# A decoder layer with sparse attention: the sample cache's compression written into the attention loop, one batch per pair, with the key and value ring over its memory

## The chip, the cores and the metric

The kernel runs on one core of one Trainium2 chip. The metric is device microseconds of one execution, as the median of several runs. Lower is better.

## What is computed

One layer of a hybrid decoder for 1024 prompt tokens and 8 sample sequences of 4 new tokens, with 2048 tokens of paged cache behind each sequence. The model width is 1024; there are 8 query heads and 2 key/value heads of 64. Everything is float32; the large products are made as three products of a high and a low part each.

```python
# both token sets (prompt, sample)
u, v_n, q_n, q_r, kcr, vcr, ks, vs, kw, vw, gate, mg = in_projection(rms_norm(x))
o_a = gmlp_mix(u, v_n, w_s, b_s)              # mixer A, chunks of 128 tokens
kc = rms_norm(compress(kc_rows, w_ck1, w_ck2, pe_k))   # 32 rows -> 1, stride 16
vc = compress(vc_rows, w_cv1, w_cv2, pe_v)
# mixer B: three softmaxes per query: compressed blocks, selected blocks, window of 512
o_b = g0 * att(q_n, kc, vc) + g1 * att(q_r, top 16 blocks) + g2 * att(q_r, window)
x = x + (sigmoid(g_a) * (o_a @ w_a) + sigmoid(g_b) * (o_b @ w_b)) @ w_out
x = x + square(relu(rms_norm(x) @ w_up)) @ w_down
...
def compress(rows, w1, w2, pe):               # rows in chunks of 16 tokens
    first, second = ch @ w1[:half], ch @ w1[half:]
    return gelu(first[:, :-1] + second[:, 1:] + pe @ w1) @ w2
```

For the prompt the rows of `compress` are made in the kernel. For the samples they are the pages of two caches, 16 pages of 128 tokens for each of 8 sequences, found through a page table. The selected and window branches of the samples read further caches in the same way.

## The kernel before

The program is one straight list of tiles and operations. A scheduler orders the instructions of each engine from it: what stands earlier in the program has the higher priority, `tc.high_priority()` lifts what it encloses, and later work is placed where an engine would otherwise be idle. On the chip each engine then runs its own list in order, so an instruction that waits holds all that stand behind it. `tc.manual_schedule(engines={SP})` fixes, for SyncE (SP), the order in which the enclosed instructions are written; other SP instructions may be placed between them. Pools of on-chip memory are a stack: a pool opened after another was released lies over its bytes, and each new tile waits for the tiles that it covers.

The stages are these. First come the projections of keys, values, gates, mixer A and the queries, until about 233 us.

Then comes the prompt attention, in 32 steps that the code calls `pairs`: 8 blocks of 128 queries times 4 pairs of heads (loop over `u`, from line 889). Pair `u` of query block qb works on 2*(qb+1) + 2*min(qb+1, 5) + 1 blocks of 128 keys, in chunks of four, 560 blocks in all; pairs 20 to 31 hold 300 of them. One step of the loop does the logits and softmax of pair `u` (`a_steps`: TensorE to bank S, VectorE maxima, ScalarE exponentials, GpSimd scaling) and, between those, the transposes and value products of pair `u-1` (`c_steps`: `T` to bank PT, `PV` to bank O, `E` at its end). `E` stores the result to `o_d` with an SP DMA (line 873). `q_trans(u + 1)` transposes the next pair's queries and at its end issues the load of the pair two further on (`q_load`, two SP DMAs).

The compression of the sample caches follows in the program (from line 958): 16 items, 8 sequences for the keys and then 8 for the values. An item loads 16 pages of 64 KB (`c_load`; SP loads 16 page numbers into registers in two `TENSOR_LOAD`s, line 923, then issues 16 DMAs, line 931) into `raw`, of which there are two. In four quarters it splits `raw` into `hl` (one ScalarE copy, one subtraction on GpSimd, or on VectorE for the first quarter) and makes six products with `w1s` into bank F, of which there is one. A chain of small operations (`comp_hidden`, `comp_out`, for keys also `comp_knorm`) ends in the copy `co`, which GpSimd stores to `c_d`. The page loads stand in a manual order of their own; the scheduler places query loads and `o_d` stores between them.

After that stand 12 blocks of a projection that depend on nothing in the attention (`fillers(W0, ...)`, 36 chunks of 24 matmuls of 352 columns into the one bank G, weights `whl` split by ScalarE and GpSimd). They serve as filling: lowest in priority, they take what TensorE has free.

The sample attention is next. The top-k part ranks the compressed blocks (`kct` is read back from `c_d`, `q_pad` spreads the sample queries, the result is `smask`). Then ten steps of `kv_load` bring 2 MB each into `ring` (two buffers, lines 1105 to 1111), with logits, softmax and values for each; another 24 chunks of filling (`fill(W1, ...)`) stand between them. The weights of W1 lie over the prompt's keys and values (pool `kvp`, released after the attention). In memory, the pools `pa` (compression) and `p2` (attention) are released together, and `fp` (filling), `ps3` (top-k) and `p3` (ring and sample softmax) lie over them, in that order.

Branch products, output projection and the MLP follow, from about 880 us to the end.

Of the kernel before, what the change touches and what calls it, by code (L numbers as in the profile page):

```python
# [26 lines left out]
NRB = 2  # L27
# [8 lines left out]
N3 = 0  # L36
# [9 lines left out]
def build(tc, a):  # L46
# [783 lines left out]
    def c_steps(u, chunks, Ps):  # L830
# [32 lines left out]
        def E():  # L863
# [9 lines left out]
            SP.dma_start(o_d[4 + pr, :, qb * 128:(qb + 1) * 128], o)  # L873

        return T, PV, E

    hp = tc.high_priority()
    hp.__enter__()
    q_load(0)
    q_load(1)  # L880
    q_trans(0)
    prev = None
    for u in range(len(pairs) + 1):
        if u == HPU:
            hp.__exit__(None, None, None)
        A, C = [], 0
        if prev:
            pu, pch, pPs = prev
            T, PV, E = c_steps(pu, pch, pPs)
            C = len(pch)  # L890
            T(0)
            T(1)
        if u < len(pairs):
            chunks, Ps, A = a_steps(u)
            prev = (u, chunks, Ps)
            A.pop(0)()
            q_trans(u + 1)
        n_a = len(A)
        for c in range(C):
            PV(c)  # L900
            T(c + 2)
            k = min(n_a, -(-n_a * (c + LEAD) // C))
            while A and n_a - len(A) < k:
                A.pop(0)()
        while A:
            A.pop(0)()
        if C:
            E()

# [48 lines left out]
    cl = Ahead([lambda w=w, b=b: c_load(w, b) for w in range(2) for b in range(8)], RAWA)  # L958
    ctxm = tc.manual_schedule(engines={mybir.EngineType.SP})
    ctxm.__enter__()  # L960
    for which in range(2):
        w1, bias, w2 = c_weights(which)
        for b in range(8):
            raw = cl()
            tg = "FG"[b % 2] if which * 8 + b < N3 else "F"
            pb = bank(tg, 1, psS)
            out = pb[:, 0:256].rearrange("p (k g r) -> p k g r", k=2, r=8)
            for qt in range(4):
                hl = pa.tile([128, 2, 16, 32], F32R, name="hl", bufs=HIB)
                cols = slice(qt * 32, (qt + 1) * 32)  # L970
                with tc.high_priority():
                    cp(hl[:, 0], raw[:, :, cols])
                    (POOL if qt else DVE).tensor_tensor(hl[:, 1], raw[:, :, cols], f(hl[:, 0]), op=OP.subtract)
                hv, lv = (hl[:, i].rearrange("p g (o k r) -> p o k g r", k=2, r=8) for i in range(2))
                for o in range(2):
                    mm(out, w1[:, 0, qt * 2 + o], hv[:, o], qt + o == 0, False)
                    mm(out, w1[:, 1, qt * 2 + o], hv[:, o], False, False)
                    mm(out, w1[:, 0, qt * 2 + o], lv[:, o], False, qt == 3 and o == 1)
            with tc.high_priority():
                g = comp_hidden(pb[:, 0:256].rearrange("p (k c) -> p k c", k=2), 128, bias, pa)  # L980
                pb2 = bank(tg, 1, psS)
                comp_out(pb2[:, 0:128], g, w2)
                if which == 0:
                    z = comp_knorm(pb2[:, 0:128], pa, gkc, 1)
                    pt = bank(tg, 1, psS)
                    PE.transpose(pt[:, 0:128], z, ident)
                    pb2 = pt
                co = small([128, 128], "co", 1, p=pa)
                cp(co, pb2[:, 0:128])
                POOL.dma_start(c_d[which, b], co)  # L990
# [563 lines left out]
```

## Time and profile before

| | us |
|---|---|
| median of 3 runs | 1826.92 |
| lowest, highest | 1823.32, 1830.13 |
| the profiled execution's own time | 1824.63 |
| its span, first to last instruction | 1822.9 |

| stretch of the profiled execution (us) | what runs |
|---|---|
| 0 to 233 | projections |
| 233 to 704 | prompt attention, compression, filling W0, top-k of the samples at its end |
| 704 to 880 | sample attention with filling W1 |
| 880 to 1823 | branch products, output projection, MLP |

The profile's page gives the busy time of each engine over the span; the windows view gives it for each stretch, with the clock that TensorE was granted (1.00 is 2.4 GHz, a mean between 0.50 and 1.00 is a mix of that and 1.2 GHz). The timeline lists an engine's instructions in order, and in brackets the idle time before one and what ended it. Matmul durations overlap, so the cost of one in a row of many is the stretch divided by the count.

### The profile page before, as it was taken

Reading aid. Unit: us, or ns where it says so; the run is one execution under the profiler, and the core shown is the slowest. Engines: PE = TensorE matmul, PEld = TensorE weight load, DVE = VectorE, ACT = ScalarE, POOL = GpSimd, SP = SyncE. Lnnn points to the kernel's source line nnn. Section 1 sums busy time; section 2 is a strip of 40 time slices with the busy share of each in tenths; the row PEclk is TensorE's granted clock in tenths of the full one; section 3 lists DMA queues with packets and bytes.
Section 4 is the critical chain, followed back from the end, with each engine's and each line's share of the span. In section 5 each row is a group of like instructions: output and inputs, shape, how many; then the busy total and the mean of one; then the engine's idle time right before and its main releaser. Section 6 shows DMA issues by size and latency. Waiting matters only on the chain.

```text
span 1822.9 us, 30327 instructions
## 1 busy us (share of the span) xinstructions
PE 1754.0 (96%) x11095; PEld 1655.3 (91%) x11095; DVE 939.5 (52%) x2371; ACT 701.7 (38%) x1681; POOL 411.3 (23%) x603
## 2 busy tenths in 40 slices
PE   8999989999999987999899999999999999999999
PEld 6877879999999965667899999999999999999998
DVE  7637867867777884124664454333333333333333
ACT  5534567777677772222422333201320122003300
POOL 3103456665566543222000220000000000000000
PEclk9999999999999997999999999999999999999999
DMA  6232453333333224665543221111111111111121
GB/s 200 94 98 64 132 161 107 112 104 96 117 89 87 70 62 143 198 188 192 176 152 108 91 70 47 47 47 47 45 38 46 47 47 47 47 47 47 47 84 59
DMA packets 157703, 168.71 MB, mean 93 GB/s; under 512 B 51825, under 2 KB 132338, under 8 KB 157554
## 3 DMA queue, kind: packets, MB, share of 16 engines
q1 hardware_dynamic: 140194, 135.77, 24.0%
q0 software_dynamic: 6464, 20.19, 3.3%
q10 hardware_dynamic: 10896, 10.82, 1.9%
q8 instruction: 87, 1.43, 0.3%
q14 instruction: 62, 0.51, 0.1%
HBM read 136.54 MB, written 29.13 MB: 91 GB/s over the span
## 4 chain that ended last, share of the span: by engine, by line
PE 83%; DVE 7%; SPq 3%; DMA 2%; ACT 2%; issue 2%; POOL 1%; ACTq 0%; DVEq 0%; POOLq 0%
PE S L73 27%; PE G L73 18%; PE PT L73 14%; PE F L73 10%; PE O L73 10%; PE PT L843 2%; SPq L931 2%; DVE PH L57 1%; SPq L923 1%; DMA ol<-o_d 1%; DMA ring<-cs 1%; DVE S L773 1%; PE PT L698 1%; ACT P L782 0%; DMA xr<-xT 0%
## 5 line engine op out<-in xcount | busy, mean ns | idle before, releaser
L73 PE MATMUL G<-big,whl 128*128 128x352 f32 x1440 | 271.1, 333 | 14.6 <-ACT whl L54 7.0
L73 PEld LDWEIGHTS G<-big,whl 128*128 128x128 f32 x1440 | 235.5, 191 | 43.4 <-issue 16.5
L54 ACT ACTIVATE whl<-wraw 128x1024 fp32r<-128x1024 f32 x100 | 106.1, 1061 | 429.7 <-PE S L73 145.8
L73 PE MATMUL S<-U,whl 128*128 128x352 f32 x864 | 201.6, 324 | 0.0
L73 PE MATMUL S<-H,whl 128*128 128x352 f32 x840 | 190.5, 324 | 0.0
L73 PE MATMUL PT<-U,whl 128*128 128x352 f32 x576 | 154.9, 324 | 0.0
L73 PEld LDWEIGHTS S<-U,whl 128*128 128x128 f32 x864 | 150.1, 188 | 0.0
L797 POOL TENSOR_SCALAR P<-P,rs 128x128 f32<-128x128 f32 (+4 forms) x272 | 132.1, 501 | 77.6 <-DVE rs L57 51.0
L73 PEld LDWEIGHTS S<-H,whl 128*128 128x128 f32 x840 | 145.0, 188 | 0.0
L73 PE MATMUL PT<-H,whl 128*128 128x352 f32 x528 | 143.2, 324 | 0.0
L782 ACT ACTIVATE P<-S,nm 128x512 f32<-128x512 f32 (+3 forms) x208 | 108.8, 532 | 24.7 <-DVE nm L57 16.8
L73 PE MATMUL S<-wt,big 128*128 128x512 f32 x408 | 104.0, 402 | 10.5 <-ACT wt L54 7.4
L57 DVE TENSOR_TENSOR PH<-PT,PH 128x512 fp32r<-128x512 f32 (+2 forms) x160 | 98.5, 618 | 28.4 <-ACT PH L54 27.7
L118 DVE TENSOR_TENSOR whl<-wraw,whl 128x1024 fp32r<-128x1024 f32 x80 | 97.8, 1222 | 14.9 <-ACT whl L54 14.9
L73 PEld LDWEIGHTS PT<-U,whl 128*128 128x128 f32 x576 | 103.3, 188 | 0.0
L73 PE MATMUL O<-PH,V 128*128 128x256 f32 x528 | 94.2, 301 | 9.3 <-DVE PH L57 9.1
L73 PE MATMUL S<-KT,QT 128*128 128x128 f32 (+3 forms) x416 | 97.6, 347 | 4.0 <-ACT P L782 3.0
L54 ACT ACTIVATE PH<-PT 128x512 fp32r<-128x512 f32 (+2 forms) x160 | 86.6, 545 | 38.4 <-PE PT L843 37.3
L73 PE MATMUL F<-H,whl 128*128 128x352 f32 x312 | 101.2, 325 | 0.0
L73 PEld LDWEIGHTS S<-wt,big 128*128 128x128 f32 x408 | 76.2, 191 | 27.4 <-ACT wt L54 7.4
L73 PE MATMUL O<-H,whl 128*128 128x352 f32 x312 | 99.1, 324 | 0.0
L73 PE MATMUL G<-H,whl 128*128 128x352 f32 x312 | 97.6, 325 | 0.5 <-DVE r L1389 0.5
(371 smaller groups left out, 3754.8 us busy)
## 6 DMA issues: line engine op xcount, KB each, us to landing
wraw<-wfm SPq DMA_DIRECT2D x80, 512.0 KB, 3.2
ring<-cs SPq DMA_DIRECT2D x128, 128.0 KB, 2.2
wraw<-wfm POOLq DMA_DIRECT2D x20, 512.0 KB, 4.2
tg<-th_d SPq DMA_DIRECT2D x48, 176.0 KB, 2.8
qdl<-qd_d SPq DMA_DIRECT2D x64, 128.0 KB, 2.6
raw<-cck SPq DMA_DIRECT2D x128, 64.0 KB, 1.9
raw<-ccv SPq DMA_DIRECT2D x128, 64.0 KB, 2.0
wtr<-wtok SPq DMA_DIRECT2D x24, 256.0 KB, 2.7
```

Source lines behind the costliest of these rows:

```text
L54: return ACT.activation(out, in_, AF.Copy, scale=scale)
L57: return DVE.tensor_tensor(out, x, y, op=op)
L73: return PE.matmul(out, l, r, start=start, stop=stop, skip_group_check=skip)
L118: (POOL if i < FM_BR else DVE).tensor_tensor(t[:, 1], raw, f(t[:, 0]), op=OP.subtract)
L698: PE.transpose(pt[:, j], src[:, j], ident)
L773: DVE.tensor_tensor_reduce(S, S, m, scale=-1.0, scalar=3e38, op0=OP.add, op1=OP.min, accum_out=dst)
L782: ACT.activation(Ps[c][:, lo:hi], Ss[c][:, lo:hi], AF.Exp, bias=nm[:, 0, k:k + 1], scale=todo[h, br, i], accum_out=sm[:, i, k:k + 1])
L797: POOL.tensor_scalar(P, P, rs[:, 1, k:k + 1], 1.0, op0=OP.mult, op1=OP.mult)
L843: PE.transpose(pt[:, j], Ps[c][:, j * 128:(j + 1) * 128], ident)
L923: _, vals = nc.values_load_multi_w_load_instructions(ptab[0:1, i0:i0 + 16], engines=[mybir.EngineType.SP], min_val=0, max_val=159, skip_ru ...
L931: SP.dma_start(dst, src)
```

## The change

Four things are changed. The compression item becomes a function `c_item(which, b)`, and the attention loop calls it at the end of step `u` for `u` from 2 to 17, so that item `u - 2` stands in the program behind pair `u`'s logits and ahead of pair `u + 1`. The manual order of SP now begins ahead of the attention loop and encloses it, with its query loads and the page loads in the order in which they are written. The `o_d` store of `E` goes from SP to GpSimd (32 DMAs of 64 KB). And `ring` gets a pool of its own, `rg`, opened first after `pa` and `p2` are released and so at the beginning of `pa`'s memory; `fp`, `ps3` and `p3` follow behind it. The second bank for early items, `N3`, was zero before and goes. The code of `page`, `page_load`, `Ahead`, `c_load` and `c_weights` is only moved.

```diff
@@ c_steps, E @@
-            SP.dma_start(o_d[4 + pr, :, qb * 128:(qb + 1) * 128], o)
+            POOL.dma_start(o_d[4 + pr, :, qb * 128:(qb + 1) * 128], o)
@@ ahead of the attention loop @@
+    ptab = consts.tile([1, 128], I32, name="ptab")
+    SP.dma_start(ptab, a["pt"])
...
+    cl = Ahead([lambda w=w, b=b: c_load(w, b) for w in range(2) for b in range(8)], RAWA)
+    cw = {}
+
+    def c_item(which, b):
+
+        if b == 0:
+            cw[which] = c_weights(which)
+        w1, bias, w2 = cw[which]
+        raw = cl()
+        pb = bank("F", 1, psS)
...
+            co = small([128, 128], "co", 1, p=pa)
+            cp(co, pb2[:, 0:128])
+            POOL.dma_start(c_d[which, b], co)
+
+    ctxm = tc.manual_schedule(engines={mybir.EngineType.SP})
+    ctxm.__enter__()
     hp = tc.high_priority()
     hp.__enter__()
     q_load(0)
@@ end of the loop body @@
         if C:
             E()
...
-    ctxm = tc.manual_schedule(engines={mybir.EngineType.SP})
-    ctxm.__enter__()
-    for which in range(2):
-        w1, bias, w2 = c_weights(which)
-        for b in range(8):
-            raw = cl()
-            tg = "FG"[b % 2] if which * 8 + b < N3 else "F"
...
+        if 2 <= u < 18:
+            c_item((u - 2) // 8, (u - 2) % 8)
+
     ctxm.__exit__(None, None, None)
     p2.release()
     pa.release()
@@ memory of the sample stage @@
     olp = pool("olp", side="right")
+    rg = pool("rg")
     fp = pool("fp")
...
-        t = p3.tile([128, 4, 4, 256], F32, name="ring", bufs=NRB)
+        t = rg.tile([128, 4, 4, 256], F32, name="ring", bufs=NRB)
...
     fp.release()
+    rg.release()
     wst0.release()
```

## Rows read from the trace of the kernel before

**Rows 1.** The page's part 1: busy us, share of span, instructions per engine.
```profile
PE 1754.0 (96%) x11095; PEld 1655.3 (91%) x11095; DVE 939.5 (52%) x2371; ACT 701.7 (38%) x1681; POOL 411.3 (23%) x603
```

**Rows 2.** Windows: length, busy us per engine (instructions), granted clock, DMA share, GB/s.
```profile
250.00:470.00 220.00, 212.94 (x1539) 207.87 (x1538) 164.71 (x568) 160.94 (x476) 135.47 (x214) 0.99 0.40 114
470.00:704.00 234.00, 212.91 (x1521) 200.21 (x1519) 182.23 (x572) 164.99 (x480) 135.00 (x226) 0.96 0.28 80
...
656.00:704.00 48.00, 34.23 (x235) 28.99 (x233) 37.43 (x118) 27.20 (x87) 20.00 (x42) 0.86 0.25 69
704.00:716.00 12.00, 7.78 (x47) 6.32 (x46) 1.51 (x6) 3.08 (x5) 7.32 (x7) 0.57 0.80 250
716.00:866.00 150.00, 140.69 (x971) 101.70 (x969) 43.98 (x109) 38.35 (x88) 32.65 (x40) 1.00 0.62 195
```

**Rows 3.** Timeline of TensorE: start, length, operation, count, idle time before it.
```profile
636.79 1.59 PE L73 MATMUL F<-hl,w1s 128*128 128x256 f32 x12
651.55 0.40 PE L73 MATMUL O<-PH,V2C 128*128 128x256 f32 x2
666.10 0.43 PE L73 MATMUL F<-kct,qp 128*32 128x128 f32 x8 [2.26 <-DMA kct<-c_d]
667.49 0.40 PE L73 MATMUL O<-PH,V2C 128*128 128x256 f32 x2
690.61 0.73 PE L73 MATMUL O<-PH,V 128*128 128x256 f32 x4 [2.69 <-DVE PH L57]
703.78 0.40 PE L73 MATMUL O<-PH,V2C 128*128 128x256 f32 x2
707.24 0.95 PE L73 MATMUL G<-big,whl 128*128 128x352 f32 x2 [3.06 <-ACT whl L54]
860.20 4.02 PE L73 MATMUL G<-big,whl 128*128 128x352 f32 x23 [0.18 <-DVE zu L57]
```

**Rows 4.** Tiles G, F's sources and co: median of one, first and last start.
```profile
L57 DVE TENSOR_TENSOR zt<-G,rep x36: 509/518/526, 260.9 to 615.6; 128x352 f32<-128x352 f32 x36
L54 ACT ACTIVATE hl<-raw x64: 614/632/682, 263.5 to 638.8; 128x512 fp32r<-128x512 f32 x64
L973 POOL TENSOR_TENSOR hl<-raw,hl x48: 1266/1284/1306, 264.7 to 642.3; 128x512 fp32r<-128x512 f32 x48
L54 ACT ACTIVATE co<-F x16: 258/277/318, 293.4 to 653.4; 128x128 f32<-128x128 f32 x16
```

**Rows 5.** SP's page loads and query loads: from the line view, then its timeline.
```profile
L923 SPq TENSOR_LOAD <-ptab x48: 967/978/1607, 247.3 to 832.1; - x48
...
248.74 0.88 SPq L931 DMA_DIRECT2D raw<-cck  x2
249.73 0.93 SPq L690 DMA_DIRECT2D qdl<-qd_d  x2
270.56 10.25 SPq L931 DMA_DIRECT2D raw<-cck  x16
452.91 1.08 SPq L690 DMA_DIRECT2D qdl<-qd_d  x2
```

**Rows 6.** Idle time of engines that ended with a raw load: us, times.
```profile
  DMA raw<-cck: 11.0, 3
  DMA raw<-ccv: 6.5, 3
```

**Rows 7.** GpSimd's DMA issues, 232 to 707 us (busy, mean ns) and in the sample stage.
```profile
L990 POOL DMA_DIRECT2D c_d<-co x16 | 9.5, 597 | 8.9 <-ACT co L54 8.7 <-issue 0.2
L1043 POOL DMA_DIRECT2D th_d<-zt x12 | 7.0, 581 | 7.7 <-ACT zt L1042 3.3 <-DMA raw<-ccv 2.7 <-ACT ch_y L448 1.7
L106 POOL DMA_DIRECT2D wraw<-wfm x20: 537/551/769, 247.4 to 801.5; - x20
L1056 POOL DMA_DIRECT2D o_d<-yt x12: 539/544/547, 807.9 to 883.9; - x12
```

**Rows 8.** SP at the end of the attention: timeline, and its longest wait.
```profile
671.34 35.63 SPq L873 DMA_DIRECT2D o_d<-o_o  x3
708.36 1.91 SPq L931 DMA_DIRECT2D ring<-cs  x4
...
SPq L873 <- POOL o_o L872: 72.9, 5, 19.2
```

**Rows 9.** Sample stage: waits for the ring, and the ranking's result with its uses.
```profile
PE S L73 <- DMA ring<-cs: 6.1, 4, 2.5
...
L1224 DVE CUSTOM_DVE_ANT_1 s_P<-S,smask x8: 691/692/693, 723.9 to 841.5; 128x512 f32<-128x512 f32 x8
L1147 DVE TENSOR_SCALAR smask<-cnt x2: 167/172/176, 687.1 to 695.7; 128x30 f32<-128x30 f32 x2
```

More of the change, by code (lines that the diff above doesn't have):

```diff
@@ L35 @@
 FM_LP = FM_BR
-N3 = 0
 LEAD = 1
@@ L872, in E @@
                 POOL.tensor_tensor(o[64 * h:64 * h + 64], t1[0:64, h], t3[:, h], op=OP.add)
-            SP.dma_start(o_d[4 + pr, :, qb * 128:(qb + 1) * 128], o)
+            POOL.dma_start(o_d[4 + pr, :, qb * 128:(qb + 1) * 128], o)
         return T, PV, E
[L877 to L908, printed above, removed]
     ptab = consts.tile([1, 128], I32, name="ptab")
@@ L958, in build @@
     cl = Ahead([lambda w=w, b=b: c_load(w, b) for w in range(2) for b in range(8)], RAWA)
+    cw = {}
[5 more added lines that the diff above has]
+        pb = bank("F", 1, psS)
+        out = pb[:, 0:256].rearrange("p (k g r) -> p k g r", k=2, r=8)
+        for qt in range(4):
+            hl = pa.tile([128, 2, 16, 32], F32R, name="hl", bufs=HIB)
+            cols = slice(qt * 32, (qt + 1) * 32)
+            with tc.high_priority():
+                cp(hl[:, 0], raw[:, :, cols])
+                (POOL if qt else DVE).tensor_tensor(hl[:, 1], raw[:, :, cols], f(hl[:, 0]), op=OP.subtract)
+            hv, lv = (hl[:, i].rearrange("p g (o k r) -> p o k g r", k=2, r=8) for i in range(2))
+            for o in range(2):
+                mm(out, w1[:, 0, qt * 2 + o], hv[:, o], qt + o == 0, False)
+                mm(out, w1[:, 1, qt * 2 + o], hv[:, o], False, False)
+                mm(out, w1[:, 0, qt * 2 + o], lv[:, o], False, qt == 3 and o == 1)
+        with tc.high_priority():
+            g = comp_hidden(pb[:, 0:256].rearrange("p (k c) -> p k c", k=2), 128, bias, pa)
+            pb2 = bank("F", 1, psS)
+            comp_out(pb2[:, 0:128], g, w2)
+            if which == 0:
+                z = comp_knorm(pb2[:, 0:128], pa, gkc, 1)
+                pt = bank("F", 1, psS)
+                PE.transpose(pt[:, 0:128], z, ident)
+                pb2 = pt
+            co = small([128, 128], "co", 1, p=pa)
+            cp(co, pb2[:, 0:128])
+            POOL.dma_start(c_d[which, b], co)
@@ L959, in build @@
     ctxm = tc.manual_schedule(engines={mybir.EngineType.SP})
     ctxm.__enter__()
-    for which in range(2):
-        w1, bias, w2 = c_weights(which)
-        for b in range(8):
-            raw = cl()
-            tg = "FG"[b % 2] if which * 8 + b < N3 else "F"
[L966 to L990, printed above, removed]
@@ new lines, in build @@
+    hp = tc.high_priority()
+    hp.__enter__()
+    q_load(0)
+    q_load(1)
+    q_trans(0)
+    prev = None
+    for u in range(len(pairs) + 1):
+        if u == HPU:
+            hp.__exit__(None, None, None)
+        A, C = [], 0
+        if prev:
+            pu, pch, pPs = prev
+            T, PV, E = c_steps(pu, pch, pPs)
+            C = len(pch)
+            T(0)
+            T(1)
+        if u < len(pairs):
+            chunks, Ps, A = a_steps(u)
+            prev = (u, chunks, Ps)
+            A.pop(0)()
+            q_trans(u + 1)
+        n_a = len(A)
+        for c in range(C):
+            PV(c)
+            T(c + 2)
+            k = min(n_a, -(-n_a * (c + LEAD) // C))
+            while A and n_a - len(A) < k:
+                A.pop(0)()
+        while A:
+            A.pop(0)()
+        if C:
+            E()
+        if 2 <= u < 18:
+            c_item((u - 2) // 8, (u - 2) % 8)
```

## The prediction

> **What bounds the kernel now.** I read the page's engine line first: TensorE is busy 96% of the span, no other engine over 52% [rows 1]. So nothing that only shortens another engine's work can pay; what can is time in which TensorE is idle or runs at its low clock. Behind 880 us the change touches nothing. The windows view therefore comes next, for the stretches that the change touches [rows 2]. From 250 to 470 us TensorE idles 7 us of 220. From 470 to 704 it idles 21 of 234, and 14 of those lie in the last 48 us, where the granted clock is also 0.86. In the 12 us after the attention it idles 4 and the clock is 0.57. In the sample stage, 716 to 866, it idles 9 of 150 at full clock. So the soft place is the end of the attention.
>
> The timeline says why [rows 3]. The last W0 filling chunk is evacuated at 615.6 us and the last compression item at 653.4 [rows 4]; the attention goes on to 703.78 with nothing to put between its steps, and TensorE waits for its own softmax and transposes (2.69 us for a split of VectorE, 2.26 us for the ranking's load). The last chunk of a pair marks the pace without cover: 651.55 to 667.49 us, 15.9 us for 27 blocks, 0.59 us a block.
>
> **Prices.** A filling chunk is 24 matmuls; 23 take 4.02 us with the tail of the last [rows 3], so I take 3.9 us; 36 chunks are 140 us. A compression item has 24 products, 12 in 1.59 us, and with three small ones I take 3.5 us; 16 are 56 us. TensorE's busy time between 250 and 704 us is 425.9 us [rows 2]; without those two and some 5 us for the ranking, 225 us remain for about 545 blocks of attention, 0.41 us a block. The attention's own pace (0.59) is longer than its TensorE work (0.41), so it needs cover to the end, and the order decides whether there is any.
>
> **The items move forward.** Before, they came one in 24.0 us ((653.4 - 293.4) / 15) [rows 4]. Now item u - 2 stands ahead of pair u + 1, so it takes TensorE time that filling had in the first half, and the filling moves to the second. What paces the first half is SP, whose queue is now in written order. An item costs it two register loads of 0.98 us and sixteen page DMAs in 10.25 us, 12.2 us, and a query load 0.95 us [rows 5], so 13.2 us a pair. The first two loads stand in step 2 and start no earlier than now, at 248.74 us, so the query load behind them goes out at 273 us instead of 249.73. From there one in 13.2 us: the load of pair 20 at 273 + 14 * 13.2 = 458, its transposes at 461 us. Now they are at 452.9 us, when SP issues the load that follows them [rows 5]. Up to 461 TensorE has 211 us: 245 blocks of attention are 100 us, the items 56, start-up idle some 10; 45 us are left, 11 chunks. From 461 us there remain 25 chunks (98 us) and 300 blocks (123 us), 221 us, against 300 * 0.59 = 177 us of the attention's own pace. So TensorE binds to the end. 461 + 221 is 682 us; with 4% idle it is 691. I take 688 us instead of 704, **-16 us**. This agrees with the loss that can be refilled: 13.8 us idle and at most 0.14 * 48 = 6.7 us of clock. Bounds: -22 and 0.
>
> **Loads just in time.** Where an engine reached a split before its pages had landed, the engines together idled 11.0 and 6.5 us, three times each [rows 6]. Now SP has hardly any slack against the items, and a ScalarE copy that waits holds the attention's exponentials behind it, then GpSimd, then TensorE. Not shown before in this density; bounds 0 and 14 items at 2 us, 28 us. I take **+6 us**, nearer to zero, since a late item only delays pages by one item and there are two buffers.
>
> **The o_d stores on GpSimd.** 32 issues at 0.58 to 0.60 us [rows 7] are 19 us of GpSimd, which is busy 58 to 62% there [rows 2]. They wait for GpSimd's own additions, so nothing new is waited for; behind each stands the scaling of the next chunk, which the transposes need. I take 0, with filling as cover; if each came onto the path, 28 stores at 0.6 us, 17 us. Below zero it can give nothing by itself. On SP the stores waited up to 19.2 us for their data [rows 8]; in the written order that would hold page and query loads, and this is what the move avoids. The Trainium skill (page "SBUF — State Buffer", section "SBUF: two separate sides") speaks against it: descriptors of a GpSimd DMA are written through a port that VectorE can hold, and its example takes about 3100 ns instead of 620. By that, an estimate, 32 stores would cost some 80 us of GpSimd more. The rows do not show it: 28 stores among busy VectorE work took 0.58 to 0.60 us on average, those of the quieter sample stage 0.54 [rows 7].
>
> **The ring.** Its two buffers (16 KB a partition each) lie over `pa`, which by the tile sizes is about 36 KB and free when the last item ends. Its loads follow the last query load in SP's order, so they can go out some 50 us before the attention ends, not at 708.36 us behind the last store [rows 8]. That takes away the first wait and some of the 6.1 us of ring waits [rows 9]: **-3 us**, bounds -6 and 0. DMA is not short: 69 GB/s in the last 48 us against 195 in the sample stage [rows 2].
>
> **The ranking.** The new order of pools puts `kct`, the masks and the sample queries over the attention's query tiles and first P buffers, which live to the last pair. So the ranking, which ended at 695.7 us beside the attention [rows 9], now begins near its end. It needed 30 us from the load's arrival at 666.1; the first mask came at 687.1. Behind it wait the masked softmax steps, the first of which was at 723.9, 20 us after the attention [rows 9]. W1 filling, 24 chunks or 94 us, covers it, as long as chunks are left. Some 5 us of TensorE waits move from the tail to behind the attention; against them stands the low clock there (0.57 over 12 us, at most 5 us), which a busy tail would lift. I take **0**, bounds -5 and +10.
>
> **Sum.** -16 + 6 + 0 - 3 + 0 = -13 us against the profiled execution's 1824.63 (span 1822.9 and 1.7 around it): 1811.6. That execution lies 2.3 us under the median of the three runs, so the forecast for a median is **1814 us**.
>
> **Rivals.**
> 1. *The items, not TensorE, pace the attention (slower).* Queries come in behind page loads, and page loads wait for `raw`, which an item frees only when its four quarters are split. With an item period p, pair 20 starts at 276 + 14p, and where too little filling is left the attention then needs 177 us. The end is 704 us again at p = 18: that is the point from which this decides, and each microsecond more costs 14. At p = 20 it is 733 us, +29; with the ring's -3 the time is 1853. For it: the first item took 30 us from its first split to `co` [rows 4]. Against it: nothing in an item is near 18 us, SP 12.2, GpSimd 3 * 1.28, ScalarE 4 * 0.63 with its small ones, TensorE 3.5; the 24 us of before were those of work placed in gaps. Chance 0.15.
> 2. *The gain is given back behind the attention (same).* The ranking starts late, W1 chunks are spent under it, and the last ring steps run without cover. It costs the upper bound, +10, and with loads at +6 the attention's -16 is gone: about 1825. For it: 30 us of ranking now lie where none lay. Against it: 94 us of filling. Chance 0.20.
> 3. *The stores hold GpSimd.* At the longest GpSimd issue, 0.77 us [rows 7], for 28 stores on the path, 22 us instead of 0: about 1836. Chance 0.04. By the figure of the Trainium skill it would be far more.
> 4. *The change does not do what it says.* The ring loads are ordered behind the ranking's loads, whose memory comes free last, and the items stay late: 1820 to 1828. Chance 0.05.
> 5. *More comes back*: no late loads, and the idle at 250 to 300 us also filled: 1790 to 1801. Chance 0.10.
>
> **How the numbers follow.** The forecast, 1801 to 1825, has 0.46. Half a per cent, 9.1 us, is about what a measurement of this kernel can tell from no change: under 1817.8 is faster, over 1836.1 slower. Of the forecast 0.39 lies under 1817.8, with rival 5 and a little of the others 0.51. Same: 0.07 of the forecast, most of rivals 2 and 4: 0.29. Slower: rival 1, half of 3, a rest: 0.20. The range, 1796 to 1838, leaves out about one half of rival 5 and most of rival 1.
>
> **What would show it.** Right: filling in G up to the last pair; the last value product of the attention at 682 to 695 us; clock near 1.00 from 650 to 700; items one in 13 to 16 us, the last before 520; ring loads before the attention's end; GpSimd stores at 0.6 us. Wrong: items over 18 us apart with TensorE idle between 280 and 470 us; ScalarE copies of `hl` waiting for `raw` in most items; G filling spent before 650 us; ring steps without G beside them after 820.

## The result and the profile after

The changed kernel is slower: 1880.2 us median (1877.27 to 1884.06) against 1827.03, a ratio of 1.0293 with an interval of 1.0271 to 1.0315. The forecast was 1814 with a range to 1838. Rival 1, the items pacing the attention, gives 753 us for the attention's end when it is worked with the item period that the chip showed; the end is at 750.8 us.

First the windows of after, in the columns of [rows 2]. The second is cut at 650 us, since the attention now ends near 750.

```profile
250.00:470.00 220.00, 198.11 (x1293) 189.98 (x1292) 116.24 (x372) 120.40 (x336) 119.33 (x170) 0.94 0.38 113
470.00:650.00 180.00, 165.20 (x1156) 152.25 (x1154) 128.09 (x450) 129.29 (x378) 113.14 (x192) 0.98 0.36 103
650.00:750.00 100.00, 83.71 (x563) 68.68 (x561) 79.87 (x285) 74.60 (x221) 49.46 (x99) 1.00 0.09 24
750.00:880.00 130.00, 115.69 (x791) 89.66 (x790) 44.24 (x104) 34.84 (x89) 34.92 (x46) 0.92 0.54 170
```

Between 250 and 750 us TensorE is busy 198.11 + 165.20 + 83.71 = 447.0 of 500 us and idle 53. Before it was busy 425.9 of 454 and idle 28 [rows 2]. So of the 46 us by which the attention ends later, some 25 are idle time and 21 are work that takes longer (some 5 more if the ranking, which lay in that stretch before and lies behind it now, is counted off). The front is where both lie: from 250 to 470 us TensorE was idle 7 us and now 22, at a clock of 0.94 instead of 0.99, and VectorE fell from 165 to 116 us. VectorE and ScalarE had less to do there: the attention was held back.

By what, the tiles say: first and last start of the items' results, of the filling's chunks, of the attention's last product, of the ranking's masks.

```profile
L53 ACT ACTIVATE co<-F x16: 257/277/284, 289.0 to 609.5; 128x128 f32<-128x128 f32 x16
L56 DVE TENSOR_TENSOR zt<-G,rep x36: 509/524/526, 263.2 to 555.8; 128x352 f32<-128x352 f32 x36
L72 PE MATMUL O<-PH,V2C x64: 278/282/415, 234.5 to 750.5; 128*128 128x256 f32 x64
L1152 DVE TENSOR_SCALAR smask<-cnt x2: 174/178/182, 783.8 to 798.2; 128x30 f32<-128x30 f32 x2
L72 PE MATMUL O<-ring,s_ph x320: 272/273/297, 803.8 to 921.6; 128*32 128x128 f32 x160
```

The items come one in (609.5 - 289.0) / 15 = 21.4 us, not one in 13.2. The filling is spent at 555.8 us (615.6 before [rows 4]), 195 us ahead of the attention's end. The masks are made after the attention, at 783.8 us, where they had come 17 us ahead of its end [rows 9]. The sample stage, from the attention's last product to the last product with the ring, takes 750.5 to 921.6 = 171 us; before it took 161. Of the 59.2 us by which the span grew (1822.9 to 1882.1) 46.6 are the attention, 10 the sample stage; behind it 2.6 are left.

SP's timeline shows the coupling. Columns: start, length, operation, count.

```profile
341.93 8.55 SPq L896 DMA_DIRECT2D raw<-cck  x16
350.58 0.93 SPq L689 DMA_DIRECT2D qdl<-qd_d  x2
364.40 8.14 SPq L896 DMA_DIRECT2D raw<-cck  x16
372.65 0.93 SPq L689 DMA_DIRECT2D qdl<-qd_d  x2
389.52 8.91 SPq L896 DMA_DIRECT2D raw<-cck  x16
398.53 2.03 SPq L689 DMA_DIRECT2D qdl<-qd_d  x2
```

SP needs some 9 us for an item's pages and one pair's queries, and then, but for one register load of 0.98 us, stands still: 351.5 to 364.4, 373.6 to 389.5. It waits for `raw` to come free. The queries of the next pair, 0.93 us of issuing, stand behind that wait. Each of the 14 items that have to wait starts its loads within 0.1 us of the end of the subtraction that last reads their buffer. So one pair's queries go out for each item, and the attention goes at the items' pace: pairs 6 to 19 are transposed 3 to 8 us after their load goes out, where before 17 to 33 us lay between the two.

And this is what an item does in those 21 us, in TensorE's timeline (bracket: idle time before and what ended it).

```profile
367.06 0.65 PE L72 MATMUL F<-hl,w1s 128*128 128x256 f32 x4
...
371.79 0.46 PE L72 MATMUL F<-w,ch_g 128*128 128x128 f32 x2 [0.80 <-DVE ch_g L449]
373.90 6.46 PE L72 MATMUL G<-big,whl 128*128 128x352 f32 x22 [1.65 <-POOL whl L117]
380.20 0.60 PE L697 MATMUL PT<-ident,qdl 128*128 128x128 f32 x4
380.63 0.60 PE L842 MATMUL PT<-ident,P 128*128 128x128 f32 x4
381.07 0.27 PE L952 MATMUL F<-ident,ck_z 128*128 128x128 f32 x1
381.10 3.43 PE L72 MATMUL G<-big,whl 128*128 128x352 f32 x20
...
385.34 1.57 PE L72 MATMUL F<-hl,w1s 128*128 128x256 f32 x12
```

One item's last product ends at 367.7 us; the next item's first, in the same bank F, starts at 385.34. Between them lie that item's small operations: gelu, a product, a norm, a transposition, `co` at 382.19. Each is short, and each has to pass through an engine that has other work ahead of it in its list: the second product is copied to `ck_z` at 372.29 us and the norm is done at 376.2, but its transposition waits until 381.07 behind 22 filling matmuls and the queries of a pair. Over the 16 items the products take 6 to 15 us from first to last, the chain from the last product's copy to `co` 10 to 19 us for keys and 5 to 10 for values; one after the other they are the period, since the next item's first product follows `co` within 3 us each time. The row of 6.46 us also shows the clock: 24 such matmuls take 4.14 us in this trace at 763.88, so 22 at full clock are 3.8. TensorE was busy 0.46 us of the 2.9 before it, and the granted clock was 0.50 from 373.9 to 377.0 us and 0.57 to 380.2, that is mostly 1.2 GHz; from there to 384.0 it was 1.00.

### The profile page after: what moved, and what is told of

Read it like the earlier page. It is cut to its first block, busy times and chain, and to the rows that moved or that the text cites. A ratio compares the mean times of both kernels' runs of the same rounds, so it can differ in the third digit from the quotient of the medians.

```text
span 1882.1 us, 30410 instructions
## 1 busy us (share of the span) xinstructions
PE 1784.2 (95%) x11095; PEld 1669.0 (89%) x11095; DVE 934.3 (50%) x2371; ACT 705.8 (38%) x1681; POOL 426.4 (23%) x635
## 4 chain that ended last, share of the span: by engine, by line
PE 59%; DVE 5%; ACT 2%; DMA 2%; SPq 2%; issue 1%; POOL 0%; ACTq 0%; DVEq 0%; POOLq 0%
PE S L72 20%; PE PT L72 12%; PE G L72 11%; PE O L72 8%; PE F L72 7%; DVE PH L56 1%; ACT P L781 1%; SPq L896 1%; PE PT L842 1%; DMA ol<-o_d 1%; DVE S L772 1%; DMA ring<-cw 1%; ACT PH L53 1%; SPq L888 0%; DVE nm L770 0%
## 5 line engine op out<-in xcount | busy, mean ns | idle before, releaser
L72 PEld LDWEIGHTS G<-big,whl 128*128 128x128 f32 x1440 | 244.5, 199 | 47.6 <-POOL whl L117 10.7
L117 DVE TENSOR_TENSOR whl<-wraw,whl 128x1024 fp32r<-128x1024 f32 x80 | 97.7, 1222 | 14.5 <-ACT whl L53 14.5
L842 PE MATMUL PT<-ident,P 128*128 128x128 f32 x560 | 91.2, 277 | 10.3 <-DVE PH L56 3.4
```

The costliest lines, as they stand in the source:

```text
L72: return PE.matmul(out, l, r, start=start, stop=stop, skip_group_check=skip)
L117: (POOL if i < FM_BR else DVE).tensor_tensor(t[:, 1], raw, f(t[:, 0]), op=OP.subtract)
L842: PE.transpose(pt[:, j], Ps[c][:, j * 128:(j + 1) * 128], ident)
```

## The experiments

Two theories stood after the result. One: SP's written order couples the attention to the items, and the attention is late because its queries stand behind pages; take them out of that order and the loss goes, wherever the items stand. The other: the items in their new place cost the engines too much, and the order of SP only shows it; then the loss stays while the items stay in the loop. To these came a question of size, what an item's 21 us are made of, and rival 2, the ranking behind the attention.

All ratios are to the kernel before, with their 95% intervals. "Pair 20" is the start of its queries' transposition, "end" the end of the attention's last value product; "period" is the distance of the items' results, first to last over 15.

| kernel | ratio | period, us | pair 20, us | last W0 chunk, us | end, us |
|---|---|---|---|---|---|
| before | 1 | 24.0 | 452.3 | 615.6 | 704.2 |
| after | 1.0293 (1.0271 to 1.0315) | 21.4 | 577.1 | 555.8 | 750.8 |
| e1, queries on ScalarE's queue | 1.0015 (0.9994 to 1.0035) | 23.9 | 465.3 | 613.8 | 699.6 |
| e2, queries out of the written order | 1.0074 (1.0050 to 1.0097) | 24.2 | 472.8 | 618.3 | 713.4 |
| e7, an item each second pair | 1.0109 (1.0092 to 1.0126) | 27.4 | 484.6 | 606.6 | 721.4 |
| e9, short chain | 1.0064 (1.0049 to 1.0080) | 14.1 | 488.5 | 611.2 | 710.4 |
| e5, small results in PT | 1.0481 (1.0463 to 1.0498) | 20.8 | 613.2 | 554.9 | 786.4 |
| e6, e5 with e1 and e4 | 1.0232 (1.0215 to 1.0249) | 17.1 | 560.7 | 574.1 | 745.3 |
| e8, before with small results in PT | 1.0575 (1.0554 to 1.0596) | see there | 452.8 | 581.3 | 669.1 |
| e4, ring back | 1.0328 (1.0293 to 1.0364) | 21.2 | 575.8 | 554.5 | 763.7 |
| e12, e1 with e4 | 1.0018 (1.0007 to 1.0029) | 23.8 | 465.5 | 613.7 | 708.5 |
| e3, items after the loop | 1.0055 (1.0039 to 1.0071) | 26.2 | 454.2 | 635.0 | 698.9 |
| e10, before with the stores alone | 1.0006 (0.9994 to 1.0018) | 26.3 | 453.7 | 636.6 | 705.9 |
| e11, before with the ring alone | 0.9965 (0.9952 to 0.9979) | 24.0 | 453.3 | 616.6 | 690.4 |

### Does SP's order hold the attention? (e1, e2, e7)

e1 takes the query loads off SP's queue and leaves all else of the change.

```diff
-                SP.dma_start(qd_t[i][:, :, d], qd_d[qb, :, pr * 256:(pr + 1) * 256].rearrange("p (a d) -> p a d", d=64))
+                ACT.dma_start(qd_t[i][:, :, d], qd_d[qb, :, pr * 256:(pr + 1) * 256].rearrange("p (a d) -> p a d", d=64))
```

> The changed kernel with one edit: the query loads are issued by ScalarE's queue and no longer by SP's. Everything else stays, the items one per pair and SP's page loads in written order. Theory A (query loads stand behind page loads on SP, page loads wait for an item to free its pages, the item's products wait on TensorE behind the next pair's query transposes: a closed loop of some 21 us a pair): the loop is open, items come one in 13 to 16 us, the attention ends at 690 to 710 us instead of 751, the time is 1815 to 1840. Theory B (an item ahead of each pair takes that long whatever loads the queries, because of its own chain through one bank F): items still 20 us or more apart, 1865 to 1885.

Measured: 1828.9 us, 1.0015. So 51 of the 53 us of the loss are gone. Pair 20 is back at 465 us and the attention's end at 699.6.

```profile
L53 ACT ACTIVATE co<-F x16: 264/279/318, 289.9 to 647.9; 128x128 f32<-128x128 f32 x16
L56 DVE TENSOR_TENSOR zt<-G,rep x36: 508/518/526, 261.1 to 613.8; 128x352 f32<-128x352 f32 x36
L72 PE MATMUL O<-PH,V2C x64: 277/282/579, 237.1 to 699.3; 128*128 128x256 f32 x64
```

The items, though, are 23.9 us apart, as in before, in spite of their early place in the program. Pairs 6 to 19 are again transposed 14 to 35 us after their load. So the attention was held by the place of the query loads behind the page loads, and the items are slow by themselves. The Trainium skill (page "DMA: Bandwidth & Descriptors", section "Issuing engines are not separate DMA queues") says that issuing from several engines saves only the time of issuing, which is usually small beside the DMA itself. This case shows another gain: the issuing of these 64 loads is 0.5 us each, some 30 us of an SP that stands still more than half of the time in the rows above, and what moving them was worth is the waits that stood ahead of them on SP.

e2 leaves them on SP but lets the scheduler place them: the written order holds only within the 16 pages of an item.

```diff
@@ ahead of the attention loop @@
-    ctxm = tc.manual_schedule(engines={mybir.EngineType.SP})
-    ctxm.__enter__()
@@ c_load @@
+        with tc.manual_schedule(engines={mybir.EngineType.SP}):
+            for pg in range(16):
+                page_load(raw[:, pg], "cc" + "kv"[which], b * 16 + pg)
```

> The changed kernel with SP's written order only inside each batch of sixteen page loads, so that the scheduler may place query loads between them, as before the change. Theory A: like the run with the query loads on ScalarE, 1815 to 1840, items 13 to 17 us apart. Theory B: 1865 to 1885, items over 20 us apart.

Measured: 1840.65 us, 1.0074; pair 20 at 472.8. Most of the loss is gone, but 12 us more of it are left than with a queue of their own. Here too the items stay 24.2 us apart.

e7 keeps the written order but asks for an item at each second pair only, so that a pair's queries have to wait for half an item.

```diff
-        if 2 <= u < 18:
-            c_item((u - 2) // 8, (u - 2) % 8)
+        if u >= 2 and u % 2 == 0:
+            c_item((u - 2) // 16, (u - 2) // 2 % 8)
```

> The changed kernel with an item at every second pair from the third, the last behind the last pair; SP's written order stays over all. Theory C: an item may take two pairs, some 28 us, which is more than its 22, so the order ties nothing; the attention ends at 700 to 715 us, the ranking is late as in the changed kernel and waits for the last item, 1830 to 1850. If the written order costs by itself, whatever the density: 1865 or more.

Measured: 1847.1 us, 1.0109. The loss falls to somewhat over a third of it with pair 20 at 484.6 us; the last item ends at 703 us, and with it the ranking comes late. The coupling whole, half and gone gives 1.029, 1.011 and 1.002; the middle one includes what the later items cost.

### What makes an item's period? (e9, e5, e6, e8)

e9 leaves the chain out: `co` is copied from the first products, without gelu, second product and norm, and the bank is free at once. What it compresses is not the layer's.

```diff
         with tc.high_priority():
-            g = comp_hidden(pb[:, 0:256].rearrange("p (k c) -> p k c", k=2), 128, bias, pa)
-            pb2 = bank("F", 1, psS)
...
-            cp(co, pb2[:, 0:128])
+            cp(co, pb[:, 0:128])
```

> The changed kernel with the end of each item left out: the hidden activation, the second product and the norm are not computed, co is copied straight from the first product in bank F (the compressed keys and values are not the reference's). What is left out is 16 times some 0.4 us of TensorE and 2 to 3 us each of ScalarE and VectorE. Theory C: bank F is held 7 to 9 us instead of 16 to 22, so items come one in 10 to 14 us, pair 20's queries are transposed at 440 to 475 us instead of 577, the filling lasts to the attention's end at 675 to 700 us, and the time is 1805 to 1835: the forecast's own sum with the item period that it assumed. Theory D (the period is the engines' load, the end of an item is no part of it): period 18 or more, 1865 or more.

Measured: 1838.6 us, 1.0064.

```profile
L53 ACT ACTIVATE co<-F x16: 259/278/324, 283.4 to 494.3; 128x128 f32<-128x128 f32 x16
L56 DVE TENSOR_TENSOR zt<-G,rep x36: 505/516/527, 256.7 to 611.2; 128x352 f32<-128x352 f32 x36
```

The period falls to (494.3 - 283.4) / 15 = 14.1 us, close to the 13.2 of the forecast, and 42 of the 53 us come back. So the chain is what made the items slow; whether by the bank it holds or by its own work, e6 tells below. But the forecast does not come true with it: pair 20 is at 488.5 us instead of 461, the filling still ends 99 us ahead of the attention, and the kernel is no faster than before. A second step was wrong, and it is taken up below. Part of the lateness has another source: in e9 SP stands in a row of query stores of the projection ahead of the first query load.

```profile
211.53 15.62 SPq L384 DMA_DIRECT2D qd_d<-qz  x5
227.19 2.65 SPq L689 DMA_DIRECT2D qdl<-qd_d  x4
```

In after that first load goes out at 210.1 us. The first pair is transposed at 231.4 instead of 215.5 us, so up to 16 us of e9's late pair 20 are this start. Why SP's order came out so in this run is open.

e5 tries to free bank F without leaving work out: the small results go to PT, a pair of banks that the attention's transpositions use.

```diff
-            pb2 = bank("F", 1, psS)
+            pb2 = bank("PT", 2, psS)
...
-                pt = bank("F", 1, psS)
+                pt = bank("PT", 2, psS)
```

> The changed kernel with one edit: the two small results at an item's end (the second product and, for keys, the transpose) go to bank PT, of which there are two, instead of the one bank F. Theory C (an item's period is what bank F is held for: 7 us of products and then 15 us of small operations for keys, 8 for values, in which the next item's products cannot start; SP's written order ties the attention to it): F is free as soon as ch_t and ch_x are read, items come one in 13 to 17 us, the attention ends at 685 to 715 us, the time is 1825 to 1850. Theory D (the items are slow because their operations stand behind the attention's on every engine, whatever bank they use): still 19 us or more an item, 1870 or more.

Measured: 1913.24 us, 1.0481, worse than after. The two slots of PT are handed on in program order, so now an attention transposition waits for the item whose result stands ahead of it, and the other way round: pair 8's queries are transposed at 383.4 us, in after at 309.1, and pairs 6 to 19 wait 29 to 50 us between load and transposition (3 to 8 in after). The period stays at 20.8, so this run does not tell the bank from the chain's work.

e6 joins e5 with the queries on ScalarE's queue (e1) and the ring back in its old place (e4, below).

```diff
-            pb2 = bank("F", 1, psS)
+            pb2 = bank("PT", 2, psS)
...
-        SP.dma_start(qd_t[i][:, :, d], qd_d[qb, :, pr * 256:(pr + 1) * 256].rearrange("p (a d) -> p a d", d=64))
+        ACT.dma_start(qd_t[i][:, :, d], qd_d[qb, :, pr * 256:(pr + 1) * 256].rearrange("p (a d) -> p a d", d=64))
...
-        t = rg.tile([128, 4, 4, 256], F32, name="ring", bufs=NRB)
+        t = p3.tile([128, 4, 4, 256], F32, name="ring", bufs=NRB)
```

> The changed kernel with three edits: the small results in bank PT, the query loads on ScalarE's queue, the ring back in the pool of the sample softmax. If theory C holds and the ring's place costs 13 us behind the attention, nothing ties the attention, the items come one in 13 to 18 us in the first half, the filling lasts to the end and the ranking runs beside the tail: 1800 to 1818, below both kernels. If theory D holds: as the run with the queries on ScalarE, 1820 to 1832.

Measured: 1867.44 us, 1.0232. Against e12, which has the same without PT (1.0018), the shared banks cost 2.1%, although the items come one in 17.1 us instead of 23.8. The chain's operations are all there in both, and with the bank free the next item's first product starts 8 to 20 us ahead of the previous `co`, where in after none starts ahead of it. So the bank did hold the items back; how much of the shorter period is the bank and how much the attention, which runs slower in e6 and leaves more room, is not split. The time lies far above both forecasts: faster items are worth nothing when the attention is tied to them by another thread.

e8 makes the edit of e5 in the kernel before, where the items stand behind the attention in the program.

```diff
-                pb2 = bank(tg, 1, psS)
+                pb2 = bank("PT", 2, psS)
...
-                    pt = bank(tg, 1, psS)
+                    pt = bank("PT", 2, psS)
```

> The kernel before with the small results of an item in bank PT. Theory C: the items, still behind the attention in the program, come closer together than 24 us (16 to 21), and more filling is left for the attention's end: 1805 to 1824. Theory D: 24 us as before, 1822 to 1832.

Measured: 1932.24 us, 1.0575.

```profile
L54 ACT ACTIVATE co<-PT x16: 277/277/278, 671.2 to 812.2; 128x128 f32<-128x128 f32 x16
L73 PE MATMUL O<-PH,V2C x64: 277/282/415, 235.9 to 668.9; 128*128 128x256 f32 x64
```

The first item's `co` is at 671.2 us, right behind the attention's last product: an item's request for PT stands behind all those of the attention. The kernel pays for it with 140 us in which the items run nearly alone. By accident this gives three figures. The attention with filling and two items ends at 669.1 us. Items with no attention beside them and their chain in PT come one in (812.2 - 671.2) / 15 = 9.4 us, about SP's time for their pages (9 us). And for each of the last 13 of them, products and chain together take 11 to 19 us from the first product to `co`: one after the other in a single bank, an estimate, they would come one in some 15 us even so, at the granted clock of 0.67 that this stretch has. The rest of the 21 to 24 us in before, after and e1 is what is added when the steps queue behind attention and filling.

### The ring and the ranking (e4, e12, e11)

e4 takes the ring's own pool out of after.

```diff
-    rg = pool("rg")
...
-        t = rg.tile([128, 4, 4, 256], F32, name="ring", bufs=NRB)
+        t = p3.tile([128, 4, 4, 256], F32, name="ring", bufs=NRB)
```

> The changed kernel with the ring back in the pool of the sample softmax, so the pools lie as before; items and SP order as changed. If the ring's place only costs the sample stage its 9 us: the attention ends near 751 us all the same, the ranking runs beside its tail, 1868 to 1880. If the ring's place causes the loss in the attention (it does not by either theory): under 1850.

Measured: 1887.55 us, 1.0328, above the 1868 to 1880 expected; the interval overlaps that of after. The masks are made at 642 and 655 us, beside the attention, whose end moves from 750.8 to 763.7; the sample stage falls from 171 to 161 us. So the pool moves some 10 us from the attention into the sample stage.

e12 does the same to e1.

```diff
-        SP.dma_start(qd_t[i][:, :, d], qd_d[qb, :, pr * 256:(pr + 1) * 256].rearrange("p (a d) -> p a d", d=64))
+        ACT.dma_start(qd_t[i][:, :, d], qd_d[qb, :, pr * 256:(pr + 1) * 256].rearrange("p (a d) -> p a d", d=64))
...
-        t = rg.tile([128, 4, 4, 256], F32, name="ring", bufs=NRB)
+        t = p3.tile([128, 4, 4, 256], F32, name="ring", bufs=NRB)
```

> The changed kernel with the query loads on ScalarE's queue and the ring back in the pool of the sample softmax. Items ahead in the program and nothing that ties the attention to them; the ranking beside the tail. If the ring's place is what the run with the queries on ScalarE still lost: 1812 to 1824. If the memory makes no difference: 1825 to 1832.

Measured: 1827.52 us, 1.0018: the end moves from 699.6 to 708.5 us, the sample stage from 168 to 158 us. Here the ring's place is worth nothing.

e11 gives the ring its pool in the kernel before, with nothing else of the change.

```diff
+    rg = pool("rg")
     fp = pool("fp")
...
-        t = p3.tile([128, 4, 4, 256], F32, name="ring", bufs=NRB)
+        t = rg.tile([128, 4, 4, 256], F32, name="ring", bufs=NRB)
```

> The kernel before with the ring in a pool of its own over the compression's memory and nothing else. If the late ranking costs the sample stage 13 us and the attention's end gains some 5 (ranking no longer beside it): 1829 to 1838, ranking done 40 us later than before. If the ring's early loads pay for it: 1818 to 1826.

Measured: 1819.34 us, 0.9965 (0.9952 to 0.9979): this part alone beats both kernels, before by 0.35%.

```profile
L73 PE MATMUL O<-PH,V2C x64: 277/282/561, 234.7 to 690.2; 128*128 128x256 f32 x64
L1148 DVE TENSOR_SCALAR smask<-cnt x2: 171/175/179, 722.7 to 737.3; 128x30 f32<-128x30 f32 x2
L931 SPq DMA_DIRECT2D ring<-cs x128: 332/333/1655, 660.1 to 836.3; - x128
L73 PE MATMUL O<-ring,s_ph x320: 272/273/298, 743.1 to 856.7; 128*32 128x128 f32 x160
```

The ring's first load goes out at 660.1 us, 48 us ahead of that of before [rows 8]. The ranking, whose memory now lies over the attention's, leaves the attention's tail: the masks are made at 722.7 us, and the attention ends at 690.2 instead of 703.9. The sample stage is 166.5 us instead of 161. 13.7 us earlier and 5.4 us longer: the last ring product is 8.3 us earlier (856.7 against 865.0), and the profiled span is 8.1 us shorter (1814.8).

### The stores (e10, e3)

e10 moves the `o_d` stores to GpSimd in the kernel before, and nothing else.

```diff
-            SP.dma_start(o_d[4 + pr, :, qb * 128:(qb + 1) * 128], o)
+            POOL.dma_start(o_d[4 + pr, :, qb * 128:(qb + 1) * 128], o)
```

> The kernel before with the 32 attention stores on GpSimd and nothing else. If a store costs its 0.6 us of GpSimd time beside other work: no difference, 1822 to 1830. If the stores make the 11 us that the kernel with the items after the loop lost: 1833 to 1839.

Measured: 1826.87 us, 1.0006: no cost. In after the 32 issues are these.

```profile
L872 POOL DMA_DIRECT2D o_d<-o_o x32: 537/586/772, 240.1 to 754.3; - x32
```

0.59 us in the middle and 0.77 at most. The example of the Trainium skill (page "SBUF — State Buffer", section "SBUF: two separate sides"), a GpSimd DMA of 620 ns that takes some 3100 ns beside a VectorE copy, does not show in any of the 32; which VectorE operations ran beside them no row here sorts out.

But e10 has another trace: the items end at 691.2 us instead of 653.4. The stores now stand in GpSimd's list, which also holds the items' subtractions. This costs nothing while the ranking's late masks (716.5 us) still meet the sample stage. It does cost in e3, which has the stores and the ring of the change, but the items behind the loop as in before.

```diff
-        if 2 <= u < 18:
-            c_item((u - 2) // 8, (u - 2) % 8)
-
+    ctxm = tc.manual_schedule(engines={mybir.EngineType.SP})
+    ctxm.__enter__()
+    for i in range(16):
+        c_item(i // 8, i % 8)
     ctxm.__exit__(None, None, None)
```

> The changed kernel with the 16 items back behind the attention loop and SP's written order for the page loads alone; the stores on GpSimd and the ring over the compression's memory stay. Both theories of the loop: items 24 us apart as before, the attention ends near 704 us. What is left is the price of the ring's place with the late ranking (0 to +10 us), the ring loads ahead (-3), and the stores (0): 1822 to 1840. If the stores or the memory were the cause of the loss, 1860 or more.

Measured: 1835.95 us, 1.0055, where stores alone gave 1.0006 and the ring alone 0.9965. GpSimd's subtractions and the ring's loads, in e3:

```profile
L939 POOL TENSOR_TENSOR hl<-raw,hl x48: 1262/1288/1322, 265.9 to 678.6; 128x512 fp32r<-128x512 f32 x48
L896 SPq DMA_DIRECT2D ring<-cs x128: 332/333/1856, 681.9 to 852.7; - x128
L72 PE MATMUL O<-ring,s_ph x320: 272/273/297, 752.1 to 873.2; 128*32 128x128 f32 x160
```

The last subtraction is at 678.6 us, in [rows 4] at 642.3; the ring over the items' memory can only be loaded then, 681.9 against 660.1 in e11; the attention ends 8.4 us later than in e11, since items still run in its tail, and the last ring product is 16.5 us later. The parts do not add up, and both lean on the end of the items. That the stores' place in GpSimd's list is what delays the items is read from e10 and e3 together; no run moved the stores alone within that list.

## Why the prediction was wrong, step by step

**The period of an item** is the step that failed first. The forecast took the engine with the most issuing time, SP, 13.2 us, as the item's period, and rival 1 was held unlikely since "nothing in an item is near 18 us". Nothing is: its longest kind of operation takes 1.3 us in the median. The period is the time that one bank is held by one item, products and chain one after the other, 21.4 us on the chip. e9 shows it (14.1 without the chain), and e6 against e12 agrees (17.1 against 23.8 with the chain in another bank). The 24.0 us of before had been put down to work placed in gaps. That was the right cause and the wrong conclusion: the gaps are as small at the new place, and e1 and e12 keep 23.9 and 23.8 us.

**Rival 1 had the mechanism and the formula.** 276 + 14 * 21.4 = 576 us for pair 20 (577.1), and 177 us for the rest uncovered (173.7): 753 us against 750.8 measured. Only its chance, 0.15, was wrong. For it stood one row, the first item with 30 us from split to result [rows 4], and it was the one row that timed an item. In e9 the formula gives 473 us with 14.1; the load of pair 20 goes out at 471, but the pair is transposed only at 488.5, so there the loads are no longer what holds it.

**What is left to cover** is the step that failed second, and e9 shows that it would have failed with items of 14 us as well. The forecast let the items take TensorE time that filling had in the first half, so that 25 chunks would be left from 461 us on, beside 300 blocks at 0.41 us of TensorE work, 221 us with some 9 of idle time. Counted over pairs 20 to 31 in each trace (a chunk is 24 products into G, an item 24 into F, at 3.9 and 3.5 us as in the prediction; "bare" is the stretch at the end that has neither filling nor items):

| kernel | from pair 20 to the end, us | chunks | items | rest, us | TensorE idle, us | of it in the bare end, and that end's length, us |
|---|---|---|---|---|---|---|
| before | 251.9 | 15.0 | 9.0 | 161.9 | 22.7 | 15.1 of 57 |
| after | 173.7 | 0 | 1.4 | 168.7 | 24.4 | 21.5 of 149 |
| e1 | 234.2 | 13.3 | 8.5 | 152.7 | 16.9 | 9.3 of 59 |
| e9 | 221.9 | 13.0 | 0.5 | 169.4 | 24.8 | 18.0 of 100 |
| e8 | 216.4 | 14.1 | 0 | 161.3 | 19.7 | 13.3 of 88 |
| e11 | 237.2 | 15.0 | 9.0 | 147.2 | 14.3 | 7.0 of 43 |
| e3 | 244.6 | 17.0 | 10.0 | 143.3 | 14.5 | 4.7 of 17 |
| e4 | 187.9 | 0 | 1.4 | 182.9 | 31.4 | 28.5 of 163 |

The counts are read from the windows view with the tile G alone, here of before (first columns: stretch, its length, busy time of TensorE with its matmuls):

```profile
452.30:704.20 251.90, 68.47 (x361) 59.29 (x360) 8.29 (x16) 0.00 (x0) 0.97 0.28 81
250.00:461.00 211.00, 95.96 (x508) 81.70 (x509) 10.91 (x21) 0.00 (x0) 0.99 0.40 115
```

The same of e9:

```profile
488.50:710.40 221.90, 59.14 (x314) 51.95 (x312) 7.28 (x14) 0.00 (x0) 0.98 0.20 60
250.00:461.00 211.00, 90.29 (x479) 76.46 (x480) 10.32 (x20) 0.00 (x0) 0.99 0.49 140
```

And with all instructions, cut where filling and items are spent, e9 and then before:

```profile
488.50:610.10 121.60, 114.81 (x784) 109.94 (x783) 77.79 (x256) 71.69 (x206) 62.09 (x109) 0.97 0.29 87
610.10:710.40 100.30, 82.28 (x544) 67.98 (x543) 77.11 (x272) 71.38 (x211) 46.91 (x93) 0.98 0.09 26
...
452.30:614.70 162.40, 157.89 (x1137) 153.44 (x1136) 122.60 (x376) 113.90 (x318) 101.31 (x160) 0.99 0.34 97
646.80:704.20 57.40, 42.25 (x290) 35.66 (x288) 45.54 (x148) 35.53 (x114) 24.50 (x50) 0.88 0.21 58
```

The cover itself does what the forecast said: where filling is at hand TensorE idles 6% (e9) and 3% (before) of the time, in the bare end 18% and 26%. Two terms were mis-sized. The first is the count: not 25 chunks but 13 were left in e9, and they were spent 100 us ahead of the end. The second is the price of a late block: in before the 162 us are some 23 of idle time, some 4 of ranking and 135 of work, 0.45 us a block; in after and e9 it is 0.48. The mean of 0.41, a subtraction over all pairs, hid that the early ones cost less ((425.9 - 229.2) less 21 chunks and 7 items, some 90 us for 245 blocks, 0.37). So these pairs, without their filling and items, take 143 to 183 us in all fourteen kernels, where the forecast had 123 and some 9 of idle time. With the forecast's own plan, pair 20 at 461 us and 25 chunks behind it, that is 702 to 742 us for the end, not 688.

Whether some order has the -16 us is not shown. In before 15 us of idle time lie in the bare end, at a clock of 0.88, which agrees with the forecast's own figure of what can be refilled. The runs that keep filling longest, e3 and e10 (chunks until 634 and 635 us, items until 682 and 684), idle less there, but 14 us ahead of pair 20 instead of 5, and they end at 698.9 and 705.9 us. No run has the items early and filling to the last pair.

**Where the filling goes.** The forecast left 11 chunks for the time up to 461 us. From 250 us on it was already 508 / 24 = 21 in before, 479 / 24 = 20 in e9 and 620 / 24 = 26 in after. The items in front did not push the filling back; in e9 the filling kept its place and the attention gave way, pair 20 from 452.3 to 488.5 us, of which the late start is up to 16. Filling takes whatever the attention leaves, so what the attention is held in the front is filling missing at its end; in after all of it was gone by 555.8 us, and pairs 20 to 31 ran bare.

**Late page loads, +6**: the idle time that ended with a raw load did not become the cost; it is 6.2 us in after against 17.5 in before [rows 6]. What was late were the queries, behind the pages. **The stores, 0**: right (1.0006 and 0.59 us), but the delay of the items behind them was not seen. **The ring**: its loads go out ahead of the attention's end, as foreseen, from 603 us in after; -3 us was small against the 6.4 us of e11, where what moves is the attention's end, by 13.7 us, from a term that the forecast had put at zero. **The ranking, 0**: of its two halves, the tail that is relieved is worth 9 to 14 us (e11, e12 and e4 each with its pair), not 5, and the sample stage pays 5 to 10, as rival 2 had it. In after the sum is 6 us to the good, within the intervals of e4.

**What would show it** did so in two signs: items over 18 us apart, and TensorE idle from 280 to 470 us (20 of 190 us, 4 in before). Filling spent before 650 us tells nothing, since before has 615.6. ScalarE's copies do not wait for `raw` in most items, and filling in G runs to 926 us beside the ring steps.

## What to carry to other kernels

Before moving a step into a loop, time one whole step from its first use of a scarce buffer to the release of that buffer, in the trace, beside its neighbours; that, not the busiest engine's share, is its period. In a queue that is written by hand, ask of each entry which event the entry ahead of it waits for: a load that costs 0.9 us to issue took on a period of 21 us from its neighbour. And before counting on filling at a late place, count in the trace how much of it is spent by then: work of the lowest priority goes into the first gaps that open, and here 21 chunks stood where the forecast left 11.

## What the runs showed of the hardware

TensorE's granted clock fell with short idle times. Behind 3.84 and 1.77 us of idle the first chunk after the attention ran slowly, and the next at full speed (TensorE's timeline of after):

```profile
754.60 0.95 PE L72 MATMUL G<-big,whl 128*128 128x352 f32 x2 [3.84 <-ACT whl L53]
757.33 5.94 PE L72 MATMUL G<-big,whl 128*128 128x352 f32 x22 [1.77 <-POOL whl L117]
...
763.88 4.14 PE L72 MATMUL G<-big,whl 128*128 128x352 f32 x24 [0.18 <-DVE yt L56]
```

22 matmuls in 5.94 us are 0.27 us each, 24 in 4.14 are 0.17. The windows of this stretch agree: the granted clock is 0.50 from 754.6 to 760.0 us, the lower level of 1.2 GHz, 0.69 from there to 763.3, and 1.00, the upper level, from 763.3 to 768.0.

```profile
754.60:760.00 5.40, 3.62 (x11) 3.17 (x12) 0.00 (x0) 1.06 (x1) 5.32 (x11) 0.50 0.93 260
760.00:763.30 3.30, 3.30 (x17) 3.28 (x16) 0.00 (x1) 0.00 (x0) 2.49 (x3) 0.69 0.99 332
763.30:768.00 4.70, 4.52 (x32) 4.06 (x34) 0.52 (x1) 1.91 (x9) 0.55 (x1) 1.00 0.43 151
```

So a stop of a few us can be paid again in the work behind it. Of the 46 us by which the attention of after ends later, 21 are longer work, not idle time. Part of that is the clock (0.94 instead of 0.99 over 220 us, at most some 11 us); what the rest is stays open.
